# Block sums of second channel weights: from a pass of their own through DRAM to the raw tiles of the units that use them

## The chip, the cores and the metric

The kernel runs on one core of a Trainium2 chip. The metric is the time of one execution on the device in microseconds, the median of several runs. TensorE (PE) multiplies matrices; VectorE (DVE) and ScalarE (ACT) work on tiles in on-chip memory; GpSimd (POOL) is nearly idle in the part that matters here; SyncE (SP) issues almost all DMAs. Each engine works through its own list of instructions in order, and an instruction that waits holds up everything behind it on that engine.

## The reference

One layer of a streaming encoder over 2048 frames of width 1024, all in float32: four mixers side by side, an output projection, and then a channel mixer. Only the channel mixer is touched by the change:

```python
h = rmsnorm(x, norm_ffn[l])
x = x + (jnp.square(jax.nn.relu(h @ w_ff1[l])) @ w_ff2[l]).astype(x.dtype)
```

`w_ff1` is 1024 x 4096 and `w_ff2` is 4096 x 1024.

## The kernel before

Both products of the channel mixer are made as block products of the Winograd form: each matrix is cut into 2 x 2 blocks, some sums of blocks are formed, and seven block products take the place of eight. Each float32 operand is also divided into a rounded high part and a low part (`split`: ScalarE copies to the high part, VectorE subtracts it), and a block product is made in three passes, high by high, high by low, low by high.

The **first product** (`ff1`, matmuls at line 1324) runs from about 1010 to 1680 us: two halves of the tokens, and in each 16 column blocks j. While block j is multiplied, the weights of block j + 1 are loaded, summed and divided, and the activated results of block j are summed into the seven left operands of the second product and stored to DRAM (`as`).

The **second product** (loop `for n in range(7)`, matmuls at line 1489) runs from about 1680 to 2326 us. For each of the seven block products n there are eight token tiles q, and for each of these 16 steps k with three matmuls of 128x512. The order of the block products is given by `AT`. Two kinds of operand are prepared during the multiplication:

- the streamed operand `st`: `s_tile` loads two raw halves `sr` from `as` (line 1457) and divides them (lines 1458 and 1459), one token tile ahead;
- the stationary operand of a block product, 16 *units* `tu[n, k]` of 128x512: `t_unit` loads a raw tile `wr` (line 1204; `raw512`, a ring of six raw tiles, `NR`) and divides it into a pair `wh`, `wl` (lines 1198 and 1199). `split2` hands out the pairs in turn: nine of the ring (`NW`) and 14 of the pool `t2p` (`NB2`), 23 in all. A pair becomes free when the last token tile of the product that uses it is done with it.

Three of the seven block products use a block of `w_ff2` as it is, and their raw tile is loaded from `w_ff2` itself. The other four, which are the fourth to seventh in the order, use sums of blocks:

- b22 - b12 + b11 (fourth), b22 - b12 (fifth), b21 - (b22 - b12 + b11) (sixth), b12 - b11 (seventh).

These sums are made by a pass of their own. `w2_load` loads quarter blocks into a tile `w2r` (line 1419; there are two, one in `t2p`, one under the tag `gain`), `w2_step` makes four subtractions in place (line 1208 through `tsub`) and stores the four results to the DRAM tensors `tt` (line 1434). There are 32 such steps, written into the loop of the second product at k = 3 and k = 11 by a count of due steps. `t_unit` loads the finished sums from `tt`.

The order of the instructions on an engine isn't that of the source. A scheduler lays them out when the kernel is built, by priority and by a model of durations, and gives out the buffers of a tag as they come free; what is written under `hi_()` has high priority. In the trace the steps of the pass begin at 1207.8 us, in the first product, and the raw tiles of a unit are loaded as soon as a raw tile is free.

Of the kernel before, what the change touches and what calls it, by code (L numbers as in the profile page):

```python
# [10 lines left out]
F32 = mybir.dt.float32  # L11
F32R = mybir.dt.float32r
# [3 lines left out]
AF = mybir.ActivationFunctionType  # L16
ALU = mybir.AluOpType
# [4 lines left out]
P = 128  # L22
T = 2048
D = 1024
# [7 lines left out]
NW = 9  # L32
# [27 lines left out]
def emit(ctx, tc, a):  # L60
    nc = tc.nc
    V, S, G, PE, SY = nc.vector, nc.scalar, nc.gpsimd, nc.tensor, nc.sync

    dram = ctx.enter_context(tc.tile_pool(name="dram", bufs=1, space=DRAM))
# [31 lines left out]
    units = [0]  # L96
# [20 lines left out]
    c1 = p1.enter_context(tc.tile_pool(name="c1", bufs=1))  # L117
# [7 lines left out]
    def psum_mm():  # L125
        return mm.tile([P, 512], F32, tag="mm", name="mm")
# [40 lines left out]
    for r in range(2):  # L167
        G.dma_start(out=sink[r * 64:(r + 1) * 64, :],
                     in_=a["attn_sinks"].rearrange("(k r) -> r k", r=2)[r].partition_broadcast(64),
# [1014 lines left out]

    NJ = DFF // (2 * P)
    as_d = [[dram.tile([P, 4, NJ, P], F32, name=f"as{i}_{h}") for h in range(2)] for i in range(7)]
    tt_d = [dram.tile([NJ, P, D], F32, name=f"tt{i}") for i in range(2)]
    tb_d = [dram.tile([P, 4, TB], F32, name=f"tb{i}") for i in range(7)]
    run(outp(3))

# [4 lines left out]
    def split(raw, pool=ring, tags=("wh", "wl"), bufs=NW):  # L1195
        h = pool.tile([P, 512], F32R, tag=tags[0], name="wh", bufs=bufs)
        l = pool.tile([P, 512], F32R, tag=tags[1], name="wl", bufs=bufs)
        S.activation(out=h, in_=raw, func=AF.Copy)  # L1198
        V.tensor_tensor(out=l, in0=raw, in1=h, op=ALU.subtract)  # L1199
        return h, l  # L1200

    def raw512(src):
        r = ring.tile([P, 512], F32, tag="wr", name="wr", bufs=NR)
        SY.dma_start(out=r.rearrange("p (k c) -> p k c", k=4) if len(src.shape) == 3 else r, in_=src)
        return r

    def tsub(o, x, y, op=ALU.subtract):
        V.tensor_tensor(out=o, in0=x, in1=y, op=op)  # L1208
# [82 lines left out]
    def w2(k, half, nd):  # L1291
        return a["w_ff2"][(2 * k + half) * P:(2 * k + half + 1) * P, nd * 512:(nd + 1) * 512]
# [101 lines left out]
    t2p = ctx.enter_context(tc.tile_pool(name="t2p", bufs=1, reuse_waits="tile"))  # L1394
# [2 lines left out]
        return t2p.tile([P, 512], F32, tag="tq", name="tq", bufs=NT2)  # L1397

    units = [0]
    NB2 = 14  # L1400

    def split2(raw):
        n = units[0] % (NW + NB2)
        units[0] += 1
        return split(raw) if n < NW else split(raw, t2p, ("vh", "vl"), NB2)

    w2s = {}  # L1410

    def w2_load(n):
        k, c = n // 2, n % 2
        if n % 2:
            t_ = c1.tile([P, 4, 256], F32, tag="gain", name="w2r")
        else:
            t_ = t2p.tile([P, 4, 256], F32, tag="w2r", name="w2r")
        for h in range(2):
            SY.dma_start(out=t_[:, 2 * h:2 * h + 2, :], in_=a["w_ff2"][(2 * k + h) * P:(2 * k + h + 1) * P, :]
                         .rearrange("p (d c) -> p d c", d=2)[:, :, c * 256:(c + 1) * 256])  # L1420
        w2s[n] = t_

    def w2_step(n):
        k, c = n // 2, n % 2
        if n + 1 < 2 * NJ:
            w2_load(n + 1)
        t_ = w2s.pop(n)
        b11, b12, b21, b22 = (t_[:, i, :] for i in range(4))
        tsub(b11, b12, b11)
        tsub(b12, b22, b12)  # L1430
        tsub(b22, b22, b11)
        tsub(b21, b21, b22)
        for h in range(2):
            SY.dma_start(out=tt_d[h][k].rearrange("p (d c) -> p d c", d=2)[:, :, c * 256:(c + 1) * 256],
                         in_=t_[:, 2 * h:2 * h + 2, :])


    AT = (0, 1, 6, 2, 3, 4, 5)
# [1 line left out]
    def t_unit(n, k):  # L1440
        i = AT[n]
        with hi_():
            if i in (0, 1, 6):
                return split2(raw512(w2(k, *((0, 0), (1, 0), None, None, None, None, (1, 1))[i])))
            h, c = ((1, 1), (0, 1), (1, 0), (0, 0))[i - 2]
            return split2(raw512(tt_d[h][k][:, c * 512:(c + 1) * 512]))

    scnt = [0]

    def s_tile(n, q):  # L1450
        with hi_():
            s_ = big.tile([P, 2, NJ, P], F32R, tag=("hh", "hl")[scnt[0] % 2], name="st")
            scnt[0] += 1
            for h in range(2):
                ks = slice(h * 8, h * 8 + 8)
                r = big.tile([P, 8, P], F32, tag="xt", name="sr", bufs=2)
                SY.dma_start(out=r, in_=as_d[AT[n]][q // 4][:, q % 4, ks, :])
                S.activation(out=s_[:, 0, ks], in_=r, func=AF.Copy)  # L1458
                V.tensor_tensor(out=s_[:, 1, ks], in0=r, in1=s_[:, 0, ks], op=ALU.subtract)  # L1459
        return s_  # L1460
# [4 lines left out]
    def finish(q, ps, acc, tb, nd):  # L1465
        b_, t0 = (q // 4) * 2 + tb, (q % 4) * P
        r = tmp2()
        SY.dma_start(out=r, in_=x1_d[b_][t0:t0 + P, nd * 512:(nd + 1) * 512])
        tsub(r, r, acc, ALU.add)
        o = tmp2()  # L1470
        tsub(o, ps, r, ALU.add)
        SY.dma_start(out=a["out"][b_ * TB + t0:b_ * TB + t0 + P, nd * 512:(nd + 1) * 512], in_=o)

    tu = {(0, k): t_unit(0, k) for k in range(NJ)}
    s_next = s_tile(0, 0)
    w2_load(0)
    done = 0
    for n in range(7):
        for q in range(8):
            st_ = s_next  # L1480
            if (n, q) != (6, 7):
                s_next = s_tile(*((n, q + 1) if q < 7 else (n + 1, 0)))
            if n < 6 and q >= 3:
                for k in (range((q - 3) * 2, (q - 2) * 2) if q < 7 else range(8, NJ)):
                    tu[n + 1, k] = t_unit(n + 1, k)
            ps = psum_mm()
            for k in range(NJ):
                for p_, (ls, lt) in enumerate(PASS):
                    PE.matmul(ps, lhsT=st_[:, ls, k, :], rhs=tu[n, k][lt], start=k == 0 and p_ == 0,  # L1489
                              stop=k == NJ - 1 and p_ == 2)  # L1490
                while k in (3, 11) and done < min(2 * NJ, (34 * (8 * n + q) + 17 * (k == 11)) // 18):
                    w2_step(done)
                    done += 1
            if n == 0:
                S.activation(out=X[:, q], in_=ps, func=AF.Copy)
            elif n == 1:
                finish(q, ps, X[:, q], 0, 0)
            elif n == 2:
                tsub(Y[:, q], ps, X[:, q], ALU.add)
            elif n == 3:  # L1500
                tsub(X[:, q], ps, X[:, q], ALU.add)
                tsub(Y[:, q], ps, Y[:, q], ALU.add)
            elif n == 4:
                tsub(X[:, q], ps, X[:, q], ALU.add)
            elif n == 5:
                finish(q, ps, X[:, q], 1, 0)
            else:
                finish(q, ps, X[:, q], 1, 1)
                finish(q, ps, Y[:, q], 0, 1)
# [27 lines left out]
```

## Time and profile before

| | |
|---|---|
| median of three runs | 2324.29 us (2323.58 to 2330.36) |
| the profiled execution | 2333.46 us, of which the span of the profile is 2331.7 us |
| TensorE, matmuls | busy 2222.9 us, 95% of the span |
| VectorE | busy 1444.6 us, 62% |
| ScalarE | busy 957.8 us, 41% |
| GpSimd | busy 185.2 us, 8% |
| DMA | 381.36 MB, mean 164 GB/s |
| granted TensorE clock, mean | 0.988 |

How to read it: a row of a table by stretches gives the stretch, its length, then for each engine the busy time and in brackets the number of instructions started, then the granted clock, the mean busy share of the 16 DMA engines and GB/s. A row of a tile's view gives line, engine, operation, output and input, the count, then the shortest, median and longest duration in ns, and the first and last start. A row of groups gives busy time and mean duration in ns, and the idle time of the engine just ahead of it with what ended it. A row of the waits gives who waited for whom, the total in us, the number of times and the longest. "SPq" and "POOLq" are the DMA queues of SyncE and GpSimd, and rows of DMA issues end with the size and the median time from issue to landing.

### The profile page before, as it was taken

What the parts mean: (1) busy time and instruction counts of PE and PEld (TensorE: products, weight loads), DVE (VectorE), ACT (ScalarE), POOL (GpSimd) and SP (SyncE); (2) the same over time, 40 slices, a digit from 0 to 9 for tenths busy, and PEclk for the clock granted to TensorE, in tenths of its full rate; (3) what the DMA queues carried; (4) which work ended last, traced back from release to release, by engine and by line L of the source; (5) the groups of instructions that cost most, each with busy time, mean ns of one, the idle gap of its engine ahead of it and who ended that gap; (6) DMA issues with size and microseconds to landing.
All of it is one profiled execution on the core that took longest, in us unless ns stands there. A gap on an engine that the chain in (4) does not pass through costs nothing. (4 is left out here: it accounts for less than half of the span.)

```text
span 2331.7 us, 32589 instructions
## 1 busy us (share of the span) xinstructions
PE 2222.9 (95%) x11460; PEld 1759.5 (75%) x11460; DVE 1444.6 (62%) x3080; ACT 957.8 (41%) x1902; POOL 185.2 (8%) x235
## 2 busy tenths in 40 slices
PE   4999999999999999999999999999999989999999
PEld 3767777777777777777787767788877767888887
DVE  4796796796689654686666676655544445344343
ACT  3343425325433432455554565555533133233121
POOL 3112212112211110000000000000000000000000
PEclk9999999999999999999999999999999999999999
DMA  6323344443543466645677788555567666354454
GB/s 171 99 83 93 97 106 126 116 113 91 147 112 95 147 202 220 216 139 168 190 215 237 217 271 247 163 149 149 171 222 230 217 221 198 100 174 143 165 172 149
DMA packets 412900, 381.36 MB, mean 164 GB/s; under 512 B 31088, under 2 KB 338384, under 8 KB 412736
## 3 DMA queue, kind: packets, MB, share of 16 engines
q1 hardware_dynamic: 411680, 377.63, 52.8%
q0 software_dynamic: 1056, 1.64, 0.6%
q8 instruction: 90, 1.47, 0.3%
q14 instruction: 74, 0.61, 0.1%
HBM read 261.77 MB, written 116.40 MB: 162 GB/s over the span
## 5 line engine op out<-in xcount | busy, mean ns | idle before, releaser
L1489 PE MATMUL mm<-wh,st 128*128 128x512 f32 x1792 | 565.4, 396 | 15.2 <-DVE st L1459 7.1
L1489 PEld LDWEIGHTS mm<-wh,st 128*128 128x128 f32 x1792 | 337.1, 189 | 100.1 <-DVE st L1459 12.3
L1489 PE MATMUL mm<-wl,st 128*128 128x512 f32 x896 | 354.2, 395 | 0.0
L1324 PE MATMUL mm<-tb,wh 128*128 128x512 f32 x1024 | 329.5, 403 | 20.5 <-ACT tp L1343 9.7
L1458 ACT ACTIVATE st<-sr 128x1024 fp32r<-128x1024 f32 x112 | 116.0, 1056 | 411.3 <-PE mm L1489 247.5
L1324 PEld LDWEIGHTS mm<-tb,wh 128*128 128x128 f32 x1024 | 193.1, 192 | 75.7 <-ACT tp L1343 15.8
L510 PE MATMUL mm<-wh,hh 128*128 128x512 f32 x512 | 213.0, 416 | 0.7 <-ACT hh L505 0.7
L105 ACT ACTIVATE wh<-wr 128x512 fp32r<-128x512 f32 x224 | 139.0, 629 | 170.5 <-PE mm L511 113.7
L512 PE MATMUL mm<-wh,hl 128*128 128x512 f32 x512 | 205.7, 402 | 0.0
L511 PE MATMUL mm<-wl,hh 128*128 128x512 f32 x512 | 204.9, 400 | 0.0
L1324 PE MATMUL mm<-tb,wl 128*128 128x512 f32 x512 | 203.8, 401 | 0.0
L1489 PEld LDWEIGHTS mm<-wl,st 128*128 128x128 f32 x896 | 168.9, 189 | 40.2 <-DVE wl L1199 0.6
L1198 ACT ACTIVATE wh<-wr 128x512 fp32r<-128x512 f32 x208 | 125.9, 625 | 122.7 <-PE mm L1324 71.5
L111 DVE TENSOR_TENSOR wl<-wr,wh 128x512 fp32r<-128x512 f32 x224 | 151.2, 692 | 35.1 <-ACT wh L105 33.7
L1324 PE MATMUL hx<-tb,wh 128*128 128x512 f32 x512 | 162.7, 396 | 5.1 <-ACT tb L1287 2.0
L1459 DVE TENSOR_TENSOR st<-sr,st 128x1024 fp32r<-128x1024 f32 x112 | 133.9, 1221 | 49.9 <-ACT st L1458 49.4
L510 PE MATMUL mm<-hh,wh 128*128 128x512 f32 x384 | 159.4, 415 | 0.0
L1199 DVE TENSOR_TENSOR wl<-wr,wh 128x512 fp32r<-128x512 f32 x208 | 138.1, 685 | 28.8 <-ACT wh L1198 28.4
L512 PE MATMUL mm<-hh,wl 128*128 128x512 f32 x384 | 152.8, 398 | 0.0
L511 PE MATMUL mm<-hl,wh 128*128 128x512 f32 x384 | 152.5, 397 | 0.0
L1208 DVE TENSOR_TENSOR w2r<-w2r 128x256 f32<-128x256 f32 x128 | 54.1, 423 | 136.9 <-DMA w2r<-in_w_ff_dram 129.5
L1324 PEld LDWEIGHTS hx<-tb,wh 128*128 128x128 f32 x512 | 96.1, 188 | 30.4 <-ACT wh L1198 3.0
(395 smaller groups left out, 3599.8 us busy)
## 6 DMA issues: line engine op xcount, KB each, us to landing
as<-tp SPq DMA_DIRECT2D x224, 256.0 KB, 2.8
sr<-as SPq DMA_DIRECT2D x112, 512.0 KB, 4.5
wr<-in_w_ff_dram SPq DMA_DIRECT2D x176, 256.0 KB, 3.8
wr<-in_w_in_dram SPq DMA_DIRECT2D x160, 256.0 KB, 3.1
wr<-in_w_out_dram SPq DMA_DIRECT2D x64, 256.0 KB, 4.0
w2r<-in_w_ff_dram SPq DMA_DIRECT2D x64, 256.0 KB, 4.2
tt<-w2r SPq DMA_DIRECT2D x64, 256.0 KB, 3.6
wr<-tt SPq DMA_DIRECT2D x64, 256.0 KB, 4.0
```

Of the source, the lines that this page charges most:

```text
L105: S.activation(out=hi, in_=raw, func=AF.Copy)
L111: (G if le == "p" else V).tensor_tensor(out=lo, in0=raw, in1=hi, op=ALU.subtract)
L510: PE.matmul(ps, lhsT=lh, rhs=rh, start=first, stop=False)
L511: PE.matmul(ps, lhsT=lh, rhs=rl, start=False, stop=False)
L512: PE.matmul(ps, lhsT=ll, rhs=rh, start=False, stop=last)
L1198: S.activation(out=h, in_=raw, func=AF.Copy)
L1199: V.tensor_tensor(out=l, in0=raw, in1=h, op=ALU.subtract)
L1208: V.tensor_tensor(out=o, in0=x, in1=y, op=op)
L1324: PE.matmul(ps, lhsT=(wh, wl)[lw][:, ks], rhs=b[lb][:, k, :], start=first and k == 0 and q == 0, stop=k == 3 and q == 2, skip_group_check= ...
L1458: S.activation(out=s_[:, 0, ks], in_=r, func=AF.Copy)
L1459: V.tensor_tensor(out=s_[:, 1, ks], in0=r, in1=s_[:, 0, ks], op=ALU.subtract)
L1489: PE.matmul(ps, lhsT=st_[:, ls, k, :], rhs=tu[n, k][lt], start=k == 0 and p_ == 0, stop=k == NJ - 1 and p_ == 2)
```

## The change

The pass (`w2_load`, `w2_step`, the tile `w2r` and its schedule in the loop) is taken out. A unit of the last four block products now loads the blocks that it needs from `w_ff2` as raw tiles and sums them in place before it is divided: three raw tiles and two sums for the fourth product, two raw tiles and one sum for the fifth to seventh. The sum of the fourth product is also stored to DRAM, by a DMA on GpSimd's queue, since the units of the sixth product need it; `tt` shrinks to that one sum. `split2` has three pairs more, 26 in all: one more of `t2p`, one made of the two tiles of the tag `xr`, and one in the tile of the tag `gain`.

```diff
-    tt_d = [dram.tile([NJ, P, D], F32, name=f"tt{i}") for i in range(2)]
+    tt_d = dram.tile([NJ, P, 512], F32, name="tt")
...
-    NB2 = 14
+    NB2 = 15
 
     def split2(raw):
-        n = units[0] % (NW + NB2)
+        n = units[0] % (NW + NB2 + 2)
         units[0] += 1
-        return split(raw) if n < NW else split(raw, t2p, ("vh", "vl"), NB2)
...
-    def w2_load(n):
...
-    def w2_step(n):
...
+        if n < NW:
+            return split(raw)
+        if n < NW + NB2:
+            return split(raw, t2p, ("vh", "vl"), NB2)
+        if n == NW + NB2:
+            return split(raw, c1, ("xr", "xr"), 2)
+        both = c1.tile([P, 2, 512], F32R, tag="gain", name="wg")
+        S.activation(out=both[:, 0], in_=raw, func=AF.Copy)
+        V.tensor_tensor(out=both[:, 1], in0=raw, in1=both[:, 0], op=ALU.subtract)
+        return both[:, 0], both[:, 1]
...
-            h, c = ((1, 1), (0, 1), (1, 0), (0, 0))[i - 2]
-            return split2(raw512(tt_d[h][k][:, c * 512:(c + 1) * 512]))
+
+            r = raw512(w2(k, *((1, 1), (1, 1), (1, 0), (0, 1))[i - 2]))
+            x = raw512(tt_d[k] if i == 4 else w2(k, *((0, 1), (0, 1), None, (0, 0))[i - 2]))
+            tsub(r, r, x)
+            if i == 2:
+                tsub(r, r, raw512(w2(k, 0, 0)), ALU.add)
+                G.dma_start(out=tt_d[k], in_=r)
+            return split2(r)
...
-    w2_load(0)
-    done = 0
...
-                while k in (3, 11) and done < min(2 * NJ, (34 * (8 * n + q) + 17 * (k == 11)) // 18):
-                    w2_step(done)
-                    done += 1
```

More of the change, by code (lines that the diff above doesn't have):

```diff
@@ L1399, in emit @@
     units = [0]
-    NB2 = 14
+    NB2 = 15
     def split2(raw):
-        n = units[0] % (NW + NB2)
+        n = units[0] % (NW + NB2 + 2)
         units[0] += 1
-        return split(raw) if n < NW else split(raw, t2p, ("vh", "vl"), NB2)
-    w2s = {}
-    def w2_load(n):
[L1413 to L1421, printed above, removed]
-    def w2_step(n):
[L1424 to L1435, printed above, removed]
+        if n < NW:
[8 more added lines that the diff above has]
+        return both[:, 0], both[:, 1]
     AT = (0, 1, 6, 2, 3, 4, 5)
```

## The prediction

> **What bounds the kernel now.** I read the share of each engine first, then TensorE's starts by stretches of the two feed-forward products, then the waits, then the chain of waits. The first and third lines of the page:
>
> ```profile
> span 2331.7 us, 32589 instructions
> PE 2222.9 (95%) x11460; PEld 1759.5 (75%) x11460; DVE 1444.6 (62%) x3080; ACT 957.8 (41%) x1902; POOL 185.2 (8%) x235
> ```
>
> TensorE is the bound, so only what TensorE waits for can be won. The second product (line 1489) runs from 1680 to 2326 us; a product is about 92 us there. The stretches, with matmuls started in the bracket behind PE, the granted clock, the share of the DMA engines and their rate:
>
> ```profile
> 1680.00:1772.00 92.00, 89.00 (x385) 71.53 (x384) 38.70 (x57) 33.94 (x49) 0.00 (x0) 1.00 0.69 217
> 1772.00:1864.00 92.00, 87.71 (x367) 69.31 (x366) 45.92 (x68) 21.19 (x25) 0.00 (x0) 0.98 0.70 232
> 1864.00:1957.00 93.00, 85.05 (x350) 65.87 (x349) 42.01 (x61) 26.08 (x32) 0.00 (x0) 0.98 0.65 206
> 1957.00:2049.00 92.00, 92.00 (x399) 74.59 (x398) 38.11 (x48) 25.83 (x33) 0.00 (x0) 1.00 0.43 137
> 2049.00:2141.00 92.00, 92.00 (x401) 74.80 (x399) 39.16 (x48) 28.67 (x39) 0.00 (x0) 1.00 0.43 138
> 2141.00:2233.00 92.00, 92.00 (x397) 74.32 (x396) 40.77 (x51) 26.29 (x35) 0.00 (x0) 1.00 0.57 188
> ```
>
> From 1957 us on TensorE has no gap at all: 399 and 401 matmuls in 184 us are 0.230 us each, 400 to a stretch of 92 us. The first three stretches lack 15, 33 and 54 of them (400 - 385, 400 - 367, 404 - 350): 102 x 0.230 = 23.5 us. Counting starts takes in the half clock after a gap (0.98). What runs there and not later is the pass that makes the block sums. Its groups, with the first and last start:
>
> ```profile
> L1208 DVE TENSOR_TENSOR w2r<-w2r x128: 410/424/428, 1213.1 to 1939.1; 128x256 f32<-128x256 f32 x128
> L1419 SPq DMA_DIRECT2D w2r<-in_w_ff_dram x64: 592/603/1508, 1207.8 to 1932.9; - x64
> L1434 SPq DMA_DIRECT2D tt<-w2r x64: 512/568/817, 1215.7 to 1939.6; - x64
> L1204 SPq DMA_DIRECT2D wr<-tt x64: 319/320/814, 1874.9 to 2231.6; - x64
> ```
>
> The pass ends at 1939.6 us, and the losses end in the stretch that holds that moment. It begins at 1207.8 us, in the first product (line 1324). The same view there:
>
> ```profile
> 1082.00:1142.00 60.00, 57.45 (x248) 45.70 (x247) 36.56 (x58) 32.81 (x57) 0.77 (x2) 0.97 0.65 192
> 1142.00:1207.00 65.00, 63.27 (x280) 50.65 (x280) 43.83 (x69) 39.25 (x69) 1.96 (x3) 1.00 0.61 184
> 1207.00:1272.00 65.00, 61.49 (x266) 49.02 (x265) 42.97 (x75) 32.74 (x57) 0.00 (x0) 0.97 0.81 242
> 1272.00:1348.00 76.00, 70.69 (x294) 55.76 (x293) 50.70 (x88) 37.53 (x65) 0.00 (x0) 0.98 0.73 221
> 1348.00:1390.00 42.00, 36.91 (x151) 27.55 (x151) 32.22 (x46) 27.94 (x41) 0.00 (x0) 1.00 0.88 270
> 1390.00:1470.00 80.00, 76.76 (x320) 60.31 (x320) 54.18 (x95) 42.88 (x75) 0.00 (x0) 0.98 0.76 227
> 1470.00:1675.00 205.00, 205.00 (x884) 165.65 (x884) 118.10 (x185) 112.57 (x188) 0.00 (x0) 1.00 0.53 154
> ```
>
> The last row gives the clean rate, 205 / 884 = 0.232 us. By it the four rows from 1207 to 1470 lack 14, 34, 30 and 25 matmuls: 3.3, 7.8, 7.0 and 5.8 us. The 7.0 us of 1348 to 1390 belong mostly to the change of the token half, which reloads all operands (0.88 of the DMA engines); the other three make 16.9 us. Before the pass the rows of 1082 and 1142 lack 11 and 0, 2.5 us in 125, so some loss is there without it.
>
> How the pass stops TensorE is in the waits of the second product (who, for whom, us in total, times, longest) and in a piece of the chain (start, length, what):
>
> ```profile
> ACT st L1458 <- DMA sr<-as: 162.3, 40, 11.6
> DVE w2r L1208 <- DMA w2r<-in_w_ff_dram: 99.1, 22, 9.7
> PEld mm L1489 <- DVE st L1459: 12.3, 12, 2.1
> ...
> 1750.12 5.62 DMA tt<-w2r
> 1755.80 3.28 DMA w2r<-in_w_ff_dram
> 1759.55 2.36 DVE st L1459 x2
> 1763.18 5.21 DMA tt<-w2r
> 1768.46 3.32 DMA w2r<-in_w_ff_dram
> ```
>
> There are two w2r tiles. A load waits on SP until an earlier store has landed (5.2 to 5.6 us), then takes 3.3 us; VectorE, in order, stands at the first subtraction, and the division of the next streamed tile (st, line 1459) stands behind it; on SP the loads of sr stand behind the load that waits. One round takes 13.06 us (1750.12 to 1763.18), a token tile 48 x 0.230 = 11.0 us: TensorE is paced by the round.
>
> **The change part by part.** Removed are 128 subtractions, 64 loads, 64 stores and the 64 loads of tt. Added are 80 sums of 128x512 (two for each of 16 units of the fourth product, one for each of 48 later), 16 stores on POOL's queue, and units that load three raw tiles (fourth product) or two (the last three): 144 loads.
>
> ```profile
> L1208 DVE TENSOR_TENSOR tq<-mm,tq 128x512 f32<-128x512 f32 x32 | 22.1, 690 | 63.6 <-PE mm L1489 63.1
> ...
> L1459 DVE TENSOR_TENSOR st<-sr,st 128x1024 fp32r<-128x1024 f32 x112 | 133.9, 1221 | 49.9 <-ACT st L1458 49.4
> ...
> sr<-as SPq DMA_DIRECT2D x112, 512.0 KB, 4.5
> wr<-in_w_ff_dram SPq DMA_DIRECT2D x176, 256.0 KB, 3.8
> ...
> tt<-w2r SPq DMA_DIRECT2D x64, 256.0 KB, 3.6
> ...
> wgr<-in_s_w_glu_dram POOLq DMA_DIRECT2D x2, 256.0 KB, 3.9
> ...
> mraw<-in_c_masks_dram POOLq DMA_DIRECT2D x1, 256.0 KB, 6.1
> ```
>
> *VectorE*: 128 x 0.424 = 54.3 us go, 80 x 0.690 = 55.2 us come: nothing in sum, but 22.1 us (32 sums) fall into the third product and 11.0 us into each of the next three. Busy 42 us of 93 becomes some 60, and 38 to 41 some 50: covered by TensorE. Without cover the 55 us would all count.
>
> *SP*: 64 x (0.603 + 0.568 + 0.320) = 95.4 us of issue go, 144 x 0.320 = 46.1 us come: hidden either way.
>
> *First product*: without the pass the 16.9 us go down to the loss of the rows before it, 2.5 us per 125, which over the 221 us of the three rows is 4.4 us. I take 12.5 us, and 1.5 us of the half change, where two rounds compete with the reload: **14 us** (bounds 0 and 20).
>
> *Second product, first three stretches*: 23.5 us, less 2.5 us for the first streamed tiles, which are loaded just when the last stores of the first product are issued: **21 us** (bounds 0 and 23.5).
>
> *Three more slots* (26 in place of 23): ten units of a product can be divided ahead in place of seven. From 1957 us on nothing is lost with 23, so this is worth 0; its cover is what the next term uses up.
>
> *New waits*: a unit of the fourth product holds r over load, two sums and store, 3.8 + 1.4 + 3.9 = 9.1 us (11.3 with the slower POOL row), and two further tiles 4.5 us each: some 18 to 20 us of slots, by six raw tiles 3.0 to 3.4 us per unit; ten units whose divided slots are free take some 34 us, three token tiles. They are all made in the third product, since the first loads for a product now go out as soon as slots are free (wr<-tt from 1874.9, over 80 us before use). On SP a load that waits for a raw tile stands ahead of the sr loads, on VectorE a sum that waits stands ahead of st: the old mechanism with six tiles for two. The bytes of the third product: 48 loads and 16 stores of 0.262 MB and 16 sr of 0.524 MB are 25.2 MB in 88.3 us (384 x 0.230), 285 GB/s. The highest short stretch:
>
> ```profile
> 1690.00:1700.00 10.00, 8.30 (x36) 6.46 (x36) 3.62 (x8) 1.65 (x4) 0.00 (x0) 1.00 0.98 327
> ```
>
> So it fits with 0.87 of the engines, and a row at 0.88 (1348 us) lost 7 us. The fifth to seventh products' units need 4.2 MB more per product (137 and 188 GB/s become some 185 and 235), where 232 went with losses but 188 without. Bounds: 0 (nothing late), and 102 x 0.230 / 16 = 1.47 us per round of the old pass, of which 16 ran there, with four transfers each, for every unit with four transfers and half for two: 23.5 + 35.2 = 58.7 us. Below nothing it can't go; gains are counted already. Near which end? A sr load has a whole token tile of slack, no unit is wanted within 11 us, and a raw tile waits for sums, not for a store, in three products of four. I take **8 us**: some 6 in the third product, 2 at the later changes of product.
>
> The rows POOL gives for 256 KB, 3.9 and 6.1 us, are the price of its store. The Trainium skill ("SBUF — State Buffer", "A bandwidth-pool intuition that's wrong") speaks against that queue: a DMA of 620 ns took some 3100 ns while a VectorE copy held the port that GpSimd needs for its descriptors. By it each of the 16 stores would be 2.5 us later, by six tiles 16 x 2.5 / 6 = 6.7 us more in the third product, an estimate from that page; by the row nothing is added. No row of this case shows a POOL DMA beside sums like these.
>
> **Sum**: -14 - 21 + 8 = -27 us. On the profiled execution, 2333.5 us (span 2331.7), that is 2306.5; the median of the three runs is 2324.3, 9.2 us below, and the sum is a difference of stalls, so I subtract it there: **2297 us**.
>
> **The rivals.**
> *All is hidden.* New waits 0, and 18 + 23.5 = 41.5 us are won: 2283 us. For it: the clean stretches from 1957 us, where sixteen unit loads come in a burst. Against: one load per unit there, not three.
> *The stall moves into the third product.* Its 16 units each cost a round's 1.47 us: -35 + 23.5 = -11.5, 2313 us. For it: 285 GB/s. Against: six tiles, and few of them wait for a store.
> *The first product's loss isn't the pass's.* Stores of sums and operand loads stay, 0.73 to 0.81 of the DMA engines now; then -21 + 8 = -13, 2311 us. Against: 0.65 at 1082 lost a quarter as much.
> *Slower: raw tiles pace four products.* In every token tile of the third to sixth product SP stands at a load whose raw tile isn't free, sr comes late, and each unit costs its share of a round: -35 + 58.7 = +24, 2348 us. It decides once these waits pass 35 us in sum, 8.8 us per product, what the first three stretches lose now (23.5 / 3 = 7.8). Against: no store lies in the round of the last three.
> *The change doesn't do what it says*: the planned order puts unit loads so that waits of 28 to 42 us come back and gain and loss cancel: 2324 us.
>
> **How the numbers follow.** Forecast 0.42, all hidden 0.18, stall moves 0.17, first product 0.10, slower 0.08, cancel 0.05. The range 2281 to 2320 takes in the first four and leaves out the last two and tails. A measurement of this kernel tells about 0.3%, 7 us, from no change. Faster beyond it are the first four less their edges, 0.85; within it 0.06; slower, with part of the cancelling, 0.09.
>
> **What would show it.** Right: some 280 matmuls in each 65 us between 1207 and 1340, and 400 in 92 us for the first two products of the second part; no VectorE wait on w2r, and ACT's wait for sr below 60 us. The third product shows the new price: a few gaps in its first three token tiles, ended by st. The forecast is wrong if gaps stand in the fifth to seventh products (raw tiles pace them), or between 1207 and 1470 without the pass, or if a sum waits for a POOL store's tile.

## The result, and the profile after

The changed kernel takes 2302.89 us (median of four runs, 2298.35 to 2307.88) against 2324.22 us before: a ratio of 0.9891, 95% interval 0.9867 to 0.9916. The forecast of 2297 us was 6 us off and the range held the time. The sum came out, but two of its terms didn't: in the profiled pair the first product won more than was forecast, and the second product won almost nothing.

The profiled execution after is 2299.8 us, with a span of 2298.0. The two profiled executions stand 33.7 us apart and the medians 21.3: that of before lay 9.2 us above its median, that of after 3.1 us below. Of the kernel before only this one execution was profiled, so which product those 9.2 us belong to isn't known.

The first and last start of one kind of matmul in each product, first the profile before, then that after; this is how the lengths of the two products are taken in all that follows:

```profile
L1324 PE MATMUL mm<-tb,wl x512: 387/396/793, 1007.8 to 1680.4; 128*128 128x512 f32 x171
L1489 PE MATMUL mm<-wh,st x1792: 387/392/628, 1680.6 to 2326.2; 128*128 128x512 f32 x200
```

```profile
L1324 PE MATMUL mm<-tb,wl x512: 388/396/760, 1003.4 to 1650.5; 128*128 128x512 f32 x171
L1472 PE MATMUL mm<-wh,st x1728: 387/392/767, 1650.7 to 2292.5; 128*128 128x512 f32 x192
```

The first product went from 672.6 to 647.1 us (25.5 less), the second from 645.6 to 641.8 (3.8 less). The remaining 4.4 us were there before the first product began, in work that the change doesn't touch.

The stretches of the profile after, of the first product and then of the second:

```profile
1082.00:1142.00 60.00, 58.58 (x260) 46.78 (x259) 39.09 (x63) 34.91 (x61) 1.10 (x2) 1.00 0.65 195
1142.00:1207.00 65.00, 64.88 (x287) 51.90 (x286) 42.70 (x68) 38.46 (x67) 1.42 (x2) 1.00 0.69 203
1207.00:1272.00 65.00, 65.00 (x288) 52.28 (x289) 40.27 (x63) 36.19 (x61) 0.00 (x0) 1.00 0.64 185
1272.00:1330.00 58.00, 57.59 (x249) 46.28 (x248) 37.58 (x56) 34.35 (x56) 0.00 (x0) 1.00 0.59 176
1330.00:1370.00 40.00, 37.43 (x155) 28.05 (x154) 31.27 (x42) 26.92 (x41) 0.00 (x0) 1.00 0.79 242
1370.00:1450.00 80.00, 80.00 (x345) 64.19 (x344) 49.31 (x78) 45.86 (x78) 0.00 (x0) 1.00 0.58 170
1450.00:1650.00 200.00, 200.00 (x864) 161.88 (x863) 114.82 (x179) 111.88 (x186) 0.00 (x0) 1.00 0.52 152
...
1650.00:1742.00 92.00, 89.12 (x382) 71.19 (x382) 40.24 (x49) 37.00 (x55) 0.00 (x0) 1.00 0.58 183
1742.00:1834.00 92.00, 92.00 (x400) 74.80 (x399) 39.81 (x49) 25.91 (x34) 0.66 (x1) 1.00 0.57 191
1834.00:1927.00 93.00, 89.28 (x378) 70.17 (x377) 51.01 (x67) 23.18 (x29) 7.56 (x14) 1.00 0.78 260
1927.00:2019.00 92.00, 90.75 (x395) 73.87 (x394) 52.13 (x70) 28.41 (x36) 0.54 (x1) 1.00 0.60 195
2019.00:2111.00 92.00, 92.00 (x397) 74.33 (x397) 48.16 (x62) 26.97 (x35) 0.00 (x0) 1.00 0.60 192
2111.00:2203.00 92.00, 84.88 (x359) 68.37 (x358) 43.53 (x56) 22.51 (x28) 0.00 (x0) 0.96 0.61 201
```

In the first product the losses of the rows from 1207 on are gone but for the change of the token half: by the clean rate (200 / 864 = 0.2315 us) the row of 1330 lacks 18 matmuls, 4.1 us, where it lacked 30. In the second product the row of 1742 is clean. By 400 matmuls to 92 us and 404 to 93, the rows of 1650, 1834, 1927, 2019 and 2111 lack 18, 26, 5, 3 and 41: 4.1, 6.0, 1.2, 0.7 and 9.4 us, 21.4 us in all. What the old pass lost in the first three stretches, the new sums mostly lose in the third to sixth.

The waits of the second product after:

```profile
ACT st L1443 <- DMA sr<-as: 89.0, 28, 9.0
ACT wh L1198 <- DVE wr L1208: 86.2, 40, 7.3
DVE wr L1208 <- DMA wr<-in_w_ff_dram: 60.0, 39, 3.8
PE mm L1472 <- DVE tq L1208: 7.1, 1, 7.1
```

The wait of VectorE on w2r (99.1 us before) is replaced by 60.0 us on the raw tiles of the sums, and ScalarE, which has to round the sum, waits 86.2 us behind them. The longest single gap of TensorE, 7.1 us, is a wait for an eviction (tq), the sum by which VectorE takes a finished tile out of one of TensorE's two result banks. VectorE's and SP's order around it, in the sixth product (start, length, engine, what, and in brackets the idle time ahead and its cause):

```profile
2137.64 0.69 DVE L1208 TENSOR_TENSOR wr<-wr 128x512 f32<-128x512 f32 x1 [1.72 <-DMA wr<-in_w_ff_dram]
2138.25 1.22 DVE L1444 TENSOR_TENSOR st<-sr,st 128x1024 fp32r<-128x1024 f32 x1
2143.25 0.69 DVE L1208 TENSOR_TENSOR wr<-wr 128x512 f32<-128x512 f32 x1 [3.78 <-DMA wr<-in_w_ff_dram]
2145.12 0.69 DVE L1208 TENSOR_TENSOR tq<-tq,X 128x512 f32<-128x512 f32 x1 [1.18 <-DMA tq<-x1d]
2145.84 0.69 DVE L1208 TENSOR_TENSOR tq<-mm,tq 128x512 f32<-128x512 f32 x1
...
2138.36 0.33 SPq L1204 DMA_DIRECT2D wr<-in_w_ff_dram  x1
2139.50 0.32 SPq L1442 DMA_DIRECT2D sr<-as  x1
2139.87 0.42 SPq L1453 DMA_DIRECT2D tq<-x1d  x1
```

A load for the next sum could be issued only when the sum at 2137.64 had freed a raw tile; it landed 4.9 us later; VectorE stood at that sum, and the eviction stood behind it. On SP the load that the eviction needs (tq<-x1d) stood behind the raw load and behind a load of sr, which was issued only when the division at 2138.25 had ended. Meanwhile both banks held finished tiles. The gaps of the third product are of the same kind: matmuls start again at 1890.89 and 1903.90 us after an eviction (Y) that stood behind sums.

### The profile page after: what moved, and what is told of

It reads as the page before. It is cut to its first block, busy times and chain, and to the rows that moved or that the text cites. A ratio compares the mean times of both kernels' runs of the same rounds, so it can differ in the third digit from the quotient of the medians.

```text
span 2298.0 us, 32485 instructions
## 1 busy us (share of the span) xinstructions
PE 2206.5 (96%) x11460; PEld 1752.5 (76%) x11460; DVE 1449.8 (63%) x3032; ACT 961.0 (42%) x1902; POOL 193.6 (8%) x251
## 5 line engine op out<-in xcount | busy, mean ns | idle before, releaser
L1472 PE MATMUL mm<-wh,st 128*128 128x512 f32 x1728 | 548.8, 395 | 14.4 <-DVE tq L1208 7.1
L1472 PEld LDWEIGHTS mm<-wh,st 128*128 128x128 f32 x1728 | 325.2, 188 | 93.3 <-issue 11.4
L1472 PE MATMUL mm<-wl,st 128*128 128x512 f32 x864 | 340.7, 394 | 0.6 <-DVE wl L1199 0.6
L1324 PE MATMUL mm<-tb,wh 128*128 128x512 f32 x1024 | 324.1, 397 | 5.1 <-DVE tp L1208 1.7
L1198 ACT ACTIVATE wh<-wr 128x512 fp32r<-128x512 f32 x204 | 124.9, 628 | 178.5 <-DVE wr L1208 86.2
L1472 PEld LDWEIGHTS mm<-wl,st 128*128 128x128 f32 x864 | 162.8, 188 | 39.4 <-DVE wl L1199 1.4
L1324 PEld LDWEIGHTS mm<-tb,wl 128*128 128x128 f32 x512 | 96.4, 188 | 22.5 <-DVE wl L1199 0.3
```

Source lines behind the costliest of these rows:

```text
L1324: PE.matmul(ps, lhsT=(wh, wl)[lw][:, ks], rhs=b[lb][:, k, :], start=first and k == 0 and q == 0, stop=k == 3 and q == 2, skip_group_check= ...
```

## The experiments

Each was timed beside the kernel before on the same chip; the ratio counts, since the kernel before took 2323.95, 2330.15 and 2325.15 us (medians) on the three chips used. "Second product" is the length from first to last start, as above.

| kernel | ratio to before, 95% interval | second product, us |
|---|---|---|
| before | 1 | 645.6 |
| after | 0.9891 (0.9867 to 0.9916) | 641.8 |
| after again, chip 1 | 0.9908 (0.9893 to 0.9923) | 644.1 |
| after again, chip 3 | 0.9900 (0.9876 to 0.9925) | 641.2 |
| before without the pass, chip 1 | 0.9873 (0.9850 to 0.9895) | 627.5 |
| raw loads on POOL's queue, chip 1 | 0.9994 (0.9977 to 1.0012) | 658.6 |
| sums on GpSimd, chip 1 | 1.0055 (1.0038 to 1.0071) | 671.5 |
| sums held behind st, chip 2 | 0.9839 (0.9823 to 0.9855) | 627.2 |
| 23 pairs, chip 2 | 0.9918 (0.9901 to 0.9935) | 647.1 |
| twelve raw tiles, chip 2 | 0.9991 (0.9976 to 1.0005) | 665.5 |
| one load per unit, chip 2 | 1.0035 (1.0022 to 1.0048) | 672.2 |
| held, second and third product too, chip 3 | 0.9833 (0.9811 to 0.9855) | 624.0 |
| held, with 23 pairs, chip 3 | 0.9867 (0.9841 to 0.9893) | 631.3 |
| held, store on SP, chip 3 | 0.9860 (0.9831 to 0.9889) | 629.4 |

**The changed kernel again.** No edit, on two chips.

> The changed kernel once more, unchanged. The profiles of before and after compare two single executions, and the four runs of after lie 9.5 us apart (2298.4 to 2307.9). Theory 1: what is left of the loss is fixed by the order of the instructions (a sum on VectorE or a load on SP that stands at a raw tile), so the median stays at 2303 us plus or minus 4 and the gap of 7.3 us at 2139 us in the seventh product's preparation comes back at the same matmul. Rival: the gap is chance in one execution, then it stands elsewhere or nowhere and the runs spread by the same 7 to 10 us.

> The changed kernel unchanged, as the measure for the three runs beside it on the same chip: 0.989 to 0.991 of the kernel before, the 7 us gap in the sixth product of the second part at the same matmul, if the order fixes it.

Medians 2302.0 and 2301.2 us. The sixth product's gap came back in both profiles with the same releaser: from the waits of the run on chip 1, and then of that on chip 3,

```profile
PE mm L1472 <- DVE tq L1208: 7.0, 1, 7.0
```

```profile
PE mm L1472 <- DVE tq L1208: 6.9, 1, 6.9
```

So it isn't chance; it is built into the order of the instructions.

**Before without the pass.** The edit takes the pass out and lets the units load a plain block; it leaves out the block sums.

```diff
-    w2_load(0)
-    done = 0
...
-                while k in (3, 11) and done < min(2 * NJ, (34 * (8 * n + q) + 17 * (k == 11)) // 18):
-                    w2_step(done)
-                    done += 1
...
-            return split2(raw512(tt_d[h][k][:, c * 512:(c + 1) * 512]))
+            return split2(raw512(w2(k, h, c)))
```

> The kernel before without the pass: no loads of w2r, no subtractions, no stores, and the units of the last four products load a plain block of w_ff2 in place of the sum, one load each as before, 23 pairs. It leaves out the block sums. Theory 1, the pass stalls both products: 35 us (14 in the first, 21 in the second product) to 45 us (21 and 23.5) less, 2279 to 2289 us. Rival, the first product's loss isn't the pass's: 21 to 23 us less, 2301 us, with gaps still between 1210 and 1470 us.

The profile (execution of 2286.23 us):

```profile
L1324 PE MATMUL mm<-tb,wl x512: 388/396/741, 1004.8 to 1651.3; 128*128 128x512 f32 x171
L1487 PE MATMUL mm<-wh,st x1792: 387/392/796, 1651.5 to 2279.0; 128*128 128x512 f32 x200
```

The first product is as long as after the change (646.5 us), so its gain is all of what the pass can give there. The second product is 627.5 us: between these profiles the pass cost it 18.1 us, and of these the changed kernel gives 14.3 back (641.8 - 627.5). The three executions without a profile were slower, 2295 to 2298 us; what they lost can't be seen, so the median of 2295.52 us lies above the expected 2279 to 2289, and this stays open. By the medians the kernel without the pass wins 28.4 us, by the two profiles 47. So 627.5 us is the length in one fast execution and not a proven floor; that the three held kernels with 26 pairs, below, have 624.0 to 629.4 us in executions within 3.1 us of their medians supports it.

**Whose order: SP's or VectorE's?** Two edits: the 144 raw loads of the sums on POOL's queue, and the 80 sums on GpSimd (one line of each shown).

```diff
-            r = raw512(w2(k, *((1, 1), (1, 1), (1, 0), (0, 1))[i - 2]))
+            r = raw512(w2(k, *((1, 1), (1, 1), (1, 0), (0, 1))[i - 2]), G)
```

```diff
-            tsub(r, r, x)
+            G.tensor_tensor(out=r, in0=r, in1=x, op=ALU.subtract)
```

> The changed kernel with the raw loads of the units that need a sum (144) issued on POOL's queue in place of SP's. Theory 1a, SP's order: sr loads and the loads for the last sums no longer stand behind a raw load, so half or more of the 17 us of the second product that are left go: 2286 to 2296 us. Theory 1b, VectorE's order: the sums still stand at their raw tiles, 2300 to 2306 us. Rival, the DMA engines' share (260 GB/s in the third product) is the limit: no change, 2303 us. Slower if a POOL load lands much later than 3.9 us.

> The changed kernel with the 80 sums on GpSimd in place of VectorE. GpSimd's sums of 128x512 took 1.13 us, of 128x256 0.80 us, so some 1.4 us each, 112 us in all, hidden. Theory 1b, VectorE's order: st no longer stands behind a sum that waits for a raw tile, half or more of the 17 us goes: 2286 to 2296 us. Theory 1a, SP's order: raw tiles come free later with slower sums, 2303 to 2310 us. Rival: if the two engines hinder each other at the on-chip memory, VectorE's 1.22 us for st grows and the time goes above 2310 us.

Both were slower than the changed kernel, by some 23 and 34 us (2325.08 and 2336.16 against 2302.0 on the same chip). For the loads no expectation held, since a POOL load landed after a median of 4.4 us, not much later; for the sums the last one did. With the loads on POOL, the third product shows VectorE in the same place, and SP free of raw loads:

```profile
1906.66 0.69 DVE L1208 TENSOR_TENSOR wr<-wr 128x512 f32<-128x512 f32 x1 [5.00 <-DMA wr<-in_w_ff_dram]
...
1912.41 0.69 DVE L1208 TENSOR_TENSOR wr<-wr 128x512 f32<-128x512 f32 x1 [3.61 <-DMA wr<-in_w_ff_dram]
1913.02 0.68 DVE L1208 TENSOR_TENSOR Y<-mm,X 128x512 f32<-128x512 f32 x1
1913.62 2.35 DVE L1444 TENSOR_TENSOR st<-sr,st 128x1024 fp32r<-128x1024 f32 x2
```

An eviction (Y) and both divisions of a streamed tile stand behind sums that wait 5.0 and 3.6 us for a load. So SP's order alone isn't the cause. With the sums on GpSimd, VectorE doesn't stand, but ScalarE does, and VectorE is slower (waits, then groups from 1842 us on):

```profile
ACT wh L1198 <- POOL wr L1427: 53.3, 31, 3.7
ACT wh L1198 <- POOL wr L1429: 37.1, 10, 7.2
PE mm L1472 <- ACT st L1443: 30.9, 5, 13.1
...
L1444 DVE TENSOR_TENSOR st<-sr,st 128x1024 fp32r<-128x1024 f32 x78 | 104.6, 1363 | 76.4 <-ACT st L1443 76.3
L1427 POOL TENSOR_TENSOR wr<-wr 128x512 f32<-128x512 f32 x63 | 87.5, 1391 | 261.8 <-DMA wr<-in_w_ff_dram 179.3 <-DMA wr<-tt 81.2 <-DVE wl L1199 0.7
L1199 DVE TENSOR_TENSOR wl<-wr,wh 128x512 fp32r<-128x512 f32 x61 | 60.7, 1014 | 48.1 <-ACT wh L1198 47.5
```

The rounding of a unit (wh) waits on ScalarE for GpSimd's sum, the rounding of the streamed tile (st) has its place behind it, and TensorE waits up to 13.1 us. In both kernels st stands behind a late operand, on one engine or the other.

**The sums held behind st.** Same loads, sums, stores and pairs, but two things in the order are changed: the sums of the first thirteen units of a product are each held behind the division of a streamed tile in VectorE's list, and the units are written two per token tile from the second tile on, where the changed kernel writes two per tile from the fourth on and eight at the last.

```diff
+            y = raw512(w2(k, 0, 0)) if i == 2 else None
+            with (tc.issue_after(last_st[0].ins) if k < 13 else ExitStack()):
+                tsub(r, r, x)
+                if i == 2:
+                    tsub(r, r, y, ALU.add)
...
+            if n < 6 and (q >= 1 if n >= 2 else q >= 3):
```

> The changed kernel with the same loads, sums, stores and pairs, but the sums of units 0 to 12 of the last four products are held behind the division of the next streamed tile (st) in VectorE's order, two units per token tile from the second on, three at the seventh. So a sum stands in the order some 8 us or more after its tiles could be loaded, and st and the evictions stand ahead of it. Theory 1b, VectorE stands at sums whose raw tiles aren't there: the 14 to 17 us of the third to sixth product go but for 2, 2286 to 2291 us, below both kernels. Rival, the rate of the DMA engines in the third product (260 GB/s) is the limit: 2298 to 2303 us.

2291.62 us on a chip where the kernel before took 2330.15, a ratio of 0.9839: below the changed kernel, and its interval is clear of the changed kernel's three. The profile:

```profile
1843.00:1932.00 89.00, 89.00 (x383) 71.71 (x382) 50.33 (x65) 23.80 (x30) 7.71 (x14) 1.00 0.75 244
1932.00:2020.00 88.00, 88.00 (x384) 71.89 (x383) 52.13 (x71) 27.01 (x35) 1.08 (x2) 1.00 0.69 228
2020.00:2110.00 90.00, 90.00 (x389) 72.62 (x388) 46.20 (x59) 26.24 (x33) 0.00 (x0) 1.00 0.57 187
2110.00:2198.00 88.00, 88.00 (x382) 71.42 (x381) 47.51 (x62) 24.82 (x32) 0.00 (x0) 1.00 0.68 227
...
ACT st L1447 <- DMA sr<-as: 31.8, 12, 4.7
DVE wr L1208 <- DMA wr<-in_w_ff_dram: 22.8, 13, 6.3
```

TensorE is busy for the whole of the third to sixth product. So VectorE's work of 46 to 52 us per product wasn't the limit. ScalarE's wait for sr falls from 89.0 to 31.8 us, though no load was moved to another queue, and VectorE's wait for raw tiles from 60.0 to 22.8.

That the DMA rate wasn't the limit can't be read from these rows alone, since loads that are spread out come at a lower rate (244 GB/s in the third product, 260 in the changed kernel). Stretches of 11 us, one token tile, of the changed kernel show more:

```profile
2010.00:2021.00 11.00, 11.00 (x50) 8.94 (x49) 8.74 (x14) 4.26 (x7) 0.00 (x0) 1.00 0.89 314
2032.00:2043.00 11.00, 11.00 (x49) 8.88 (x48) 9.15 (x14) 3.91 (x5) 0.00 (x0) 1.00 0.94 314
2142.00:2153.00 11.00, 6.32 (x19) 5.08 (x20) 5.63 (x7) 1.29 (x2) 0.00 (x0) 0.69 0.73 245
```

314 GB/s are carried with TensorE full, and the stretch with the longest gap has 245: the rate doesn't by itself stop TensorE. The order of the loads and sums was the cause. Which of the two changes pays, the hold or the even spread of the units, isn't shown: no run has only one of them.

**More room, less traffic.** Twelve raw tiles in place of six (with 23 pairs, for space), and one load per unit, summed with itself (it leaves out the second and third block and the load of the stored sum); one line of each is shown:

```diff
-            x = raw512(tt_d[k] if i == 4 else w2(k, *((0, 1), (0, 1), None, (0, 0))[i - 2]))
+            x = rawx(tt_d[k] if i == 4 else w2(k, *((0, 1), (0, 1), None, (0, 0))[i - 2]))
```

```diff
-            tsub(r, r, x)
+            tsub(r, r, r)
```

> The changed kernel with twelve raw tiles in place of six (the second and third block of a sum go to six tiles of their own) and 23 pairs in place of 26. Theory 1c, the raw tiles pace the sums: with twice as many the loads run a round ahead and the third to sixth product lose 2 to 6 us in place of 15, 2288 to 2294 us. Rival 1b, the order: the planner puts the sums still earlier, as its model lets the loads come sooner, and VectorE stands at them as before, 2300 us or more. Rival DMA rate: 2303 us.

> The changed kernel with all 80 sums and 16 stores, but each unit loads one raw tile and sums it with itself; it leaves out the second and third block and the load of the stored sum (80 loads less). If the added loads are the price, the third to sixth product lose 0 to 3 us, 2286 to 2292 us. If VectorE's added 55 us is the price: 2300 to 2304 us.

Twelve raw tiles gave 2328.47 us, as the rival that names the order had it (2300 or more); the missing pairs don't explain it, since 23 pairs with six raw tiles are at 0.9918, below. One load per unit came out as neither expectation said, 2335.62 us: slower than the kernel before, with 80 loads less than the changed kernel. The likely reading is that the planner (the scheduler that lays out the lists when the kernel is built) lays out as many units ahead as it has tiles for. With one load, the sums of many units stand ahead of an eviction; VectorE's order in the third product:

```profile
1851.01 0.68 DVE L1208 TENSOR_TENSOR tq<-tq,X 128x512 f32<-128x512 f32 x1
1851.98 1.99 DVE L1208 TENSOR_TENSOR wr<-wr 128x512 f32<-128x512 f32 x3 [0.29 <-DMA wr<-in_w_ff_dram]
...
1855.03 4.30 DVE L1208 TENSOR_TENSOR wr<-wr 128x512 f32<-128x512 f32 x7
1859.24 1.22 DVE L1443 TENSOR_TENSOR st<-sr,st 128x1024 fp32r<-128x1024 f32 x1
1860.38 2.49 DVE L1199 TENSOR_TENSOR wl<-wr,wh 128x512 fp32r<-128x512 f32 x4
1862.79 0.68 DVE L1208 TENSOR_TENSOR tq<-mm,tq 128x512 f32<-128x512 f32 x1
```

Ten sums, two divisions of st and four of units stand between the two halves of a finish (the sum tq<-tq,X and the eviction tq<-mm,tq), and TensorE waits 15.2 us for the second. With twelve raw tiles the same happens on SP: loads for many units stand ahead of sr, whose longest wait grew from 9.0 to 16.9 us:

```profile
ACT st L1448 <- DMA sr<-as: 96.1, 20, 16.9
```

**The three pairs.** The changed kernel with 23 pairs, and the held one with 23.

```diff
-    NB2 = 15
+    NB2 = 14
...
-        n = units[0] % (NW + NB2 + 2)
+        n = units[0] % (NW + NB2)
```

> The changed kernel without the three more pairs: 23 as before (14 in the second pool, none of xr and gain). Prediction's step: the three pairs are worth nothing, 2299 to 2307 us. Rival, the pairs hide part of the new waits, since three units less can be divided ahead and each then holds its raw tile until the last token tile: 2308 to 2315 us.

> after_st with 23 pairs in place of 26. If the pairs are worth nothing once VectorE doesn't stand at raw tiles (the prediction's step): 0.984, as after_st, every product after the first at 88 to 90 us. If they carry part of the gain, the products that need two raw tiles per unit take 1 to 5 us more and the ratio is 0.986 to 0.990.

0.9918 against 0.9900 and 0.9908, and 0.9867 against 0.9839: the intervals overlap both times, so the times don't part the pairs from nothing. The second product is 3.0 to 5.9 us longer without them than in the three profiles of the changed kernel, and 4.1 us longer than in the held one. In both kernels with 23 pairs TensorE waits for a unit's rounding, 2.9 and 3.7 us in the second token tile of the second product and 2.7 and 1.5 us in the fourth product; in the two with 26 it waits so for 0.8 us at most. The pairs seem worth some 4 us, which the times don't show.

**The store's queue, and the other two products.** The held kernel with its store on SP, and the held kernel with the units of the second and third product held too.

```diff
-                G.dma_start(out=tt_d[k], in_=r)
+                SY.dma_start(out=tt_d[k], in_=r)
```

```diff
+                with (tc.issue_after(last_st[0].ins) if n and k < 13 else ExitStack()):
+                    return split2(raw512(w2(k, *((0, 0), (1, 0), None, None, None, None, (1, 1))[i])))
```

> after_st with the 16 stores of the fourth product's sum on SP's queue in place of POOL's. On SP a store waits for its sum and the loads of sr stand behind it: third product 1 to 6 us more, 0.985 to 0.987 of the kernel before, if POOL's queue is worth what the change makes of it. Rival: a store that stands behind its sum in a planned order costs nothing, 0.984.

> after_st with the units of the second and third product held behind st in the same way (the division's subtraction, two units per token tile). In after_st the first product still took 94.3 us where 88.7 are clean; its units for the next product are loaded in a burst just when the first streamed tiles are. Theory, the burst stands ahead of sr and st: 3 to 5 us less than after_st, 0.982 of the kernel before. Rival, the first tiles come late by themselves (their loads follow the last stores of the first part): 0.984 as after_st.

The store on SP: 0.9860, an interval that overlaps with the held kernel's, the second product 2.2 us longer; not told apart. Holding the first units too: 2285.66 us, ratio 0.9833, against 0.9839 on another chip. Its second product is 624.0 us, 3.2 less than held alone, the amount expected of the burst, but the ratios don't show it. Its ratio is the lowest of the kernels run, though not told apart from that of the held kernel: about 15.5 us below the changed kernel on the same chip (2285.66 against 2301.2), with the whole computation.

## Why the prediction was right, and where its terms were wrong

**What bounds the kernel now: right.** The pass cost both products time: without it the first takes 646.5 us in place of 672.6, the second 627.5 in place of 645.6, in one profiled execution each.

**First product, 14 us: too small in the profiled pair.** It won 25.5 us in the profiled pair, 19.4 of it after 1207 us (23.9 lost before, 4.5 after). The step that failed is the allowance: 4.4 us were left for losses like those before the pass, and the rows from 1207 to 1330 and from 1370 on lack almost none; and the change of the half won 2.9 us, not 1.5. Some 4 us more lie before 1207 us, where the pass hadn't begun (248 matmuls in the row of 1082 before, 260 after). These stay open: the kernel without the pass has 260 there too, but nothing shows what the pass could have done so early. The row of 1082 was also misread as a sign of DMA load: it alone lost 2.5 us in 60, more than half the rate of the rows with the pass and not a quarter, and after the change it loses nothing at the same 0.65 of the DMA engines. How much of the 25.5 us is chance isn't known: the first product takes 646.5 to 652.2 us in the thirteen other profiles, but its 672.6 before stand on the one execution that lay 9.2 us above its median.

**Second product, gross 21 us: nearly right.** The profile without the pass puts it at 18.1.

**New waits, 8 us: mis-sized.** They measured 14.3 us (641.8 - 627.5; 13.7 and 16.6 in the repeats). The mechanism was named, a sum on VectorE ahead of st, a raw load on SP ahead of sr, and so was the third product, with 6.0 us where some 6 were forecast. What failed is the sentence on the later products, "a raw tile waits for sums, not for a store, in three products of four", from which 2 us followed: the sixth alone lost 9.4, 7.1 of it in one wait. A round of load and sum without any store is as long as 5.6 us (4.9 and 0.7), and the planner put eight such sums between two evictions (from 2122 to 2143 us). In the third product the gaps stood at the start of the fifth to seventh token tile, not in the first three. The 14.3 us are against a kernel with 23 pairs; one without the pass and with 26 wasn't run.

**Three pairs, 0: not refuted by the times.** The profiles speak for 3 to 6 us, with waits for a unit's rounding where the pairs are missing.

**VectorE's 55 us and the DMA rate: hidden, as said.** The held kernel carries both with TensorE full.

**POOL's store.** The prediction's estimate from figures of the Trainium skill ("SBUF — State Buffer", "A bandwidth-pool intuition that's wrong") made each store some 2.5 us later. The stores landed after a median of 4.3 us in the profile after, where the pass's stores on SP took 3.6:

```profile
tt<-wr POOLq DMA_DIRECT2D x16, 256.0 KB, 4.3
```

That is 0.7 us, not 2.5, beside VectorE's two-input sums; no run here has the copy that the page speaks of, so carrying its figure over to these sums is what the estimate had wrong. SP was no better place for the store, as far as the times tell.

**The rivals.** "The stall moves into the third product" was the nearest: it moved, but to the third and the sixth. A larger gain elsewhere covered it, so that the total came near the forecast is in part luck, two errors of opposite sign: in the profiled pair the first product won 11.5 us more than forecast (25.5, not 14), the second 9.2 us less (3.8, not 13). By the medians the kernel won 21.3 us of the 27 forecast; if the second product's 3.8 us hold there too, the rest won 17.5, 3.5 more than forecast.

**Its own signs.** No wait on w2r, the matmuls between 1207 and 1330 us (288 and 249) and the second product's row of 1742 (400) came out as said. Three signs didn't: the row of 1650 has 382 and not 400, ScalarE's wait for sr is 89.0 us and not below 60, and the sixth product has the gap that was named as a sign that raw tiles pace the later products.

## What to carry to other kernels

When a wait on a transfer is removed by moving the work elsewhere, look at which engine's list the new consumer stands in and what stands behind it: here the same work cost some 14 us when its sums were laid out as early as a model thought their tiles would be there, and nothing that the profiles show when the units were spread evenly and most sums were held behind the next thing that TensorE needs. More buffers, fewer loads and another queue didn't help here, since the layout followed them; in the traces they put more work ahead of the urgent instruction. A forecast by terms should be checked term by term afterwards, since a good total can hide two wrong ones.

## What the runs showed of the hardware that was not expected

Sums on GpSimd slow VectorE. While they ran, VectorE's division of a unit took 1014 ns on average in place of 686, and that of a streamed tile 1363 in place of 1221. The Trainium skill ("SBUF — State Buffer", "SBUF: two separate sides") says that a VectorE operation with two on-chip inputs and a GpSimd operation that reads on-chip memory take a shared pair of ports in turn, whole instructions at a time; the rows agree: the shortest division of a unit there still took 0.68 us, the longest 3.29. GpSimd's sum took 1391 ns on average where VectorE's took 690.

A gap of TensorE costs more than itself, and the trace shows by how much. In the stretch with the 7.1 us wait the granted clock is 0.96 and 41 matmuls are lacking, 9.4 us. In slices of 1 us the clock is 1.00 until 2144 us, 0.50 to 0.58 from there to 2151 and 1.00 again behind it; the gap lies from 2139.6 to 2146.7 us. So 4.3 us of matmuls ran at half the clock and lost some 2.2 us, which with the 7.1 us makes 9.3. The gaps of at most 1.0 us in the third product left the clock of their stretch at 1.00.
